# A decoder layer on one core: held-back gate products, a running sum in PSUM, low parts by adding transfers, and one more channel at seven products for eight

## The chip, the core and the metric

The kernel runs on one core of one Trainium2 chip. The core has a matrix engine (TensorE, PE here; the loading of its stationary operand has its own row, PEld), VectorE (DVE), ScalarE (ACT), GpSimd (POOL) and SyncE (SP), which issues most transfers from HBM. POOL issues the rest, among them all those that add what they bring to what is already in SBUF (the on-chip memory of 128 partitions). PE writes to PSUM, whose banks hold 512 float32 numbers for each partition.

The metric is the device time of one execution in microseconds; smaller is better. Beside it stands a profiled execution of the same program.

## What is computed

One layer over 512 tokens of 1024 channels: a normalisation, one wide input projection, two mixers (a convolution module A and gated linear attention B), a gated merge, an output projection with residual, and a feed-forward part. What the change touches, cut from the reference:

```python
u = _rmsnorm(h, norm1_g[l])
proj = u @ w_in[l]
a_glu, q, k, v, r, g_low, gate_a, gate_b = _split_cols(proj)
...
c = jax.nn.silu(_layernorm(c, conv_ln_g[l], conv_ln_b[l]))
...
o = o.reshape(bsz, seq, GLA_VDIM).astype(x.dtype) * jax.nn.silu(r)
y_gla = o @ w_gla_out[l]
merged = jax.nn.sigmoid(gate_a) * y_conv + jax.nn.sigmoid(gate_b) * y_gla
h = h + merged @ w_o[l]

u2 = _rmsnorm(h, norm2_g[l])
z = _causal_dwconv(u2 @ w_ffn_up[l], ffn_dw_w[l], ffn_dw_b[l])
h = h + (jax.nn.silu(z[..., :FFN_DIM]) * z[..., FFN_DIM:]) @ w_ffn_down[l]
```

D_MODEL is 1024, FFN_DIM 2816, and all inputs are float32.

## The kernel before

**Products in three passes.** Each operand is split into a high part, rounded to the type that PE multiplies fast (fp32r), and a low part, what the rounding left. A product is then three matmuls (`mm3`, L523): low x high, high x low, high x high. So PE needs a weight's low part first. `split_weight` (L400) makes both parts of the next weight in `order`: ACT casts the high part (L412, L442), and the low part is made in one of three ways. As a rule DVE subtracts (L413, L450). For the weights in the set `ADDED` (L47) ACT writes the negative of the weight, rounded, to the low tile (L444) and POOL issues a transfer that adds the weight from HBM once more (L445). Two early ones go to POOL. High and low tiles have four buffers each, raw weights four (`raw_tile`, L306). `weight` (L468) keeps the splits two entries ahead of use.

**Seven products for eight.** Where two halves of the tokens meet two halves of the channels, a Strassen-like scheme (steps a11, a12, s1, n2, s4, n3, a22) saves one product in eight for sums and differences of operands. `seven` (L1434) does it for whole weight blocks (w_r, w_o, w_down). `two_tiles` (L1325) does it for a pair of column tiles, a "two-product channel" in the feed-forward part: four weight parts x1, x3, x2, x4 (the first to the fourth), with steps a11 and a12, then n2 and s1, then n3 and s4, then a22. Each step is 12 matmuls of 256 tokens. A part's weights come from `two_sums` (L381): after the first part is split, POOL adds three half tiles (L384), after the second one more. The token sums that the steps take as the other operand (n2, s1, n3, s4) are made on DVE (L1288) and split there (L1301) in four rounds, one after each of the first channels (`some_sums`).

**The w_r stage.** `seven("w_r", ...)` makes the output gate r. `put_r` (L1525) takes each result from its bank: for a11, s1 and n2 ACT copies it to an r tile; for a12, s4 and n3 DVE combines bank and r tile (L1535), ACT applies silu (L1536) and DVE multiplies the attention output with it (L1537); for a22 ACT applies silu straight from the bank (L1531) and DVE multiplies. `gated_o` (L1229) then transposes the product on PE into one of three "ax" banks, from which ACT takes the high part and DVE the low part (L1241).

**Layer norm of branch A.** `ln_center` (L1014) subtracts the mean from one of eight channel tiles (DVE, L1015), squares it on ACT into a `btmp` tile (two buffers, L1017) and adds the square to a running sum, itself in the other `btmp` (DVE, L1021). This chain runs beside the merge's products (`pair_7`).

**The feed-forward part.** w_up has 44 column tiles, i and 22 + i for the two factors of channel tile i. `GROUPS` (L34) cuts the 22 channels into three groups of pairs; each group is made (up), then multiplied with its block of w_down. The first of a pair is gated, split and kept; the second is gated and combined with it (`first_gated` L1728, `second_of_pair` L1739). `up_plan` (L189) writes the order within a group: a plain channel is its two tiles of 24 matmuls of 512 tokens each, then its role; a unit mixes the four parts of one two-product channel with the tiles of a plain one. The main loop (L1830) walks this plan. In the first group channels 0 and 2 open, then 1, 3 and 4 are plain, then come units of channel 6 with plain 5 and of 7 with plain 8. When a two-product channel's last part is done, its value (the taps of the short convolution, silu) is begun at once.

**Order.** The text gives priorities; the builder puts each engine's instructions in a fixed order by these and by what it reckons will be ready. `tc.issue_after(x)` makes what is traced inside it follow x on x's engine; `tc.keep_in_program_order` does so among those it marks.

Of the kernel before, what the change touches and what calls it, by code (L numbers as in the profile page):

```python
# [10 lines left out]
F32 = mybir.dt.float32  # L11
# [6 lines left out]
P = 128  # L18
# [30 lines left out]
POOLED = {("w_qk", 0), ("w_qk", 1)}  # L49
ADDED -= POOLED  # L50
RATE = 5.0
ROWS = (0, 5, 5, 5, 8, 8, 8, 8)
# [48 lines left out]
def trunk_layer(ctx: ExitStack, tc: tile.TileContext, a: dict, out: bass.AP):  # L101
# [34 lines left out]
    def btmp():  # L136
        return tp.tile([P, T], F32, tag="btmp", name=nm("btmp"), bufs=2)
# [51 lines left out]
    def up_plan(gi):  # L189


        pairs = GROUPS[gi]
        whole = range(KT)

        def halves(*cuts):
            return [range(a, b) for a, b in zip((0, *cuts), (*cuts, KT))]

        def unit(q, f, kind):

            a, b = f, FT + f  # L200
            x1, x3, x2, x4 = (("part", q, part) for part in ("x1", "x3", "x2", "x4"))
            a1, a2 = (("tile", a, ks) for ks in halves(4))
            if kind == "opens":
                b1, b2, b3 = (("tile", b, ks) for ks in halves(4, 6))
                seq = [a1, x1, a2, x3, b1, x2, b2, x4, ("second", q), b3]
            elif kind == "closes":
                a1, a2, a3 = (("tile", a, ks) for ks in halves(3, 6))
                seq = [x1, a1, x3, a2, x2, a3, x4, ("second", q), ("tile", b, whole)]
            else:
                a1, a2 = (("tile", a, ks) for ks in halves(5))  # L210
                b1, b2 = (("tile", b, ks) for ks in halves(4))
                seq = [x1, a1, x3, a2, x2, b1, x4, ("second", q), b2]
            return seq + [("first", f)]

        firsts = [p for p, _ in pairs[1:]]
        if gi + 1 < len(GROUPS):
            firsts.append(GROUPS[gi + 1][0][0])
        plan = []
        n = 0
        if gi == 0:  # L220
            (p, q), (f, _) = pairs[1:3]
            for i, role in ((p, "first"), (q, "second"), (f, "first")):
                plan += [("tile", i, whole), ("tile", FT + i, whole), (role, i)]
            n = 2
        while n < len(firsts):
            last = n + 1 == len(firsts) and gi + 1 < len(GROUPS)
            kind = "closes" if last else "opens" if n == 0 else ""
            plan += unit(pairs[n][1], firsts[n], kind)
            n += 1
        if n < len(pairs):  # L230
            q = pairs[n][1]
            plan += [("tile", q, whole), ("tile", FT + q, whole), ("second", q)]
        return plan
# [97 lines left out]
    def load_block(name, pairs, step, d):  # L331
# [682 lines left out]
    def ln_center(k):  # L1014
        nc.vector.tensor_tensor(conv[k], stat["mean"], conv[k], ALU.add)  # L1015
        sq = btmp()
        nc.scalar.activation(sq, conv[k], AF.Square)  # L1017
        if k == 0:
            stat["sq"] = sq
        else:  # L1020
            nc.vector.tensor_tensor(stat["sq"], stat["sq"], sq, ALU.add)  # L1021

# [494 lines left out]

    rt = {}
    urgent += s4 + of_s4 + n3 + of_n3
# [5 lines left out]
    def put_r(step, t, n, acc):  # L1525
        if step in ("a11", "s1", "n2"):
            rt[t, n] = rp_.tile([P, T], F32, tag="r", name=nm("r"), bufs=8)
            return nc.scalar.copy(rt[t, n], acc)
        if step == "a22":
            rt[t, n] = rp_.tile([P, T], F32, tag="r", name=nm("r"), bufs=8)  # L1530
            nc.scalar.activation(rt[t, n], acc, AF.Silu)  # L1531
        else:
            r = rt[t, n]
            one, two = (r, acc) if step == "n3" else (acc, r)
            done = nc.vector.tensor_tensor(r, one, two, ALU.add if step == "a12" else ALU.subtract)  # L1535
            nc.scalar.activation(r, r, AF.Silu)  # L1536
        nc.vector.tensor_tensor(ot[t, n], ot[t, n], rt[t, n], ALU.mult)  # L1537
        return done if step == "n3" else None
# [289 lines left out]
    banks, values, units = {}, {}, {}  # L1828
    third = []
    for gi, pairs in enumerate(GROUPS):  # L1830
# [26 lines left out]
        for what, i, *rest in up_plan(gi):  # L1857
# [7 lines left out]
            if what == "part":  # L1865
# [115 lines left out]
```

## Time and profile before

| | us |
|---|---|
| median of 3 runs | 820.95 |
| lowest to highest | 820.51 to 821.41 |
| the profiled execution | 821.88 |
| its span | 820.2 |
| PE busy, share of the span | 808.7, 99% |
| DVE | 707.2, 86% |
| ACT | 488.2, 60% |
| POOL | 196.8, 24% |

The span goes from the first instruction to the last. An engine's busy time is the union of its instructions; matmuls overlap in their pipeline, so their rate is read from start to start and not from their durations. In the list of waits a row names who waited for whom, then the total, the times and the longest. In a timeline each row has the start, the time taken, engine, line, operation, what is written from what, the shapes and how many; what stands in brackets is the idle time before it and who ended it. In a table by stretches each engine has its busy time and its count. The stages in the profile: start and first projections to 245 us, w_r to 290, merge to 410, w_o to 466, and the three groups of the feed-forward part from 471, 609 and 701 us to the end.

### The profile page before, as it was taken

The numbers are of one execution on the slowest core, as the hardware profiler recorded it, in microseconds if no ns is written. First come the engines' busy times: TensorE is split into PE (matmuls) and PEld (weight loads), VectorE is DVE, ScalarE is ACT, GpSimd is POOL, SyncE is SP. The second block draws the span as 40 slices with busy tenths as digits, with TensorE's granted clock in tenths as the row PEclk, the third lists the DMA queues.
The fourth block names the chain that finished last, engine by engine and source line by source line (L and its number), as shares of the span: only waits on it lengthen the run. The fifth ranks groups of instructions, "written<-read, shape, count | busy, mean of one in ns | idle before, by whom it ended". The sixth has DMA issues, their size and how long they took to land.

```text
span 820.2 us, 11465 instructions
## 1 busy us (share of the span) xinstructions
PE 808.7 (99%) x4227; PEld 695.5 (85%) x4227; DVE 707.2 (86%) x1105; ACT 488.2 (60%) x744; POOL 196.8 (24%) x176
## 2 busy tenths in 40 slices
PE   9999999999999999999999999999999999999996
PEld 8888888888888788889988898898889988899885
DVE  6879999998999878595789889979975999689895
ACT  6667788677547574384445646556435663466554
POOL 2025433332203332122001100230123311522012
PEclk9999999999999999999999999999999999999999
DMA  8488858655831332433458613146632346335662
GB/s 327 153 193 177 190 161 178 157 123 134 183 96 36 96 111 95 129 103 103 155 106 227 201 58 103 52 159 166 140 130 92 143 121 167 103 103 178 156 129 103
DMA packets 36472, 113.60 MB, mean 139 GB/s; under 512 B 3688, under 2 KB 8944, under 8 KB 36416
## 3 DMA queue, kind: packets, MB, share of 16 engines
q1 hardware_dynamic: 28912, 86.39, 31.0%
q0 software_dynamic: 7488, 26.48, 18.9%
q8 instruction: 33, 0.54, 0.3%
q14 instruction: 23, 0.19, 0.1%
q10 hardware_dynamic: 16, 0.00, 0.0%
HBM read 110.76 MB, written 2.10 MB: 138 GB/s over the span
## 4 chain that ended last, share of the span: by engine, by line
PE 62%; DVE 1%; ACT 0%; issue 0%; POOL 0%; POOLq 0%; ACTq 0%
PE mm L527 14%; PE mm L528 14%; PE mm L529 14%; PE cv L527 4%; PE cv L528 4%; PE cv L529 4%; PE ax L529 2%; PE ax L527 2%; PE ax L528 2%; DVE btmp L1021 0%; PE ax L608 0%; PE ax L1233 0%; DVE wlo L413 0%; ACT junk L1778 0%; DVE hres L1485 0%
## 5 line engine op out<-in xcount | busy, mean ns | idle before, releaser
L527 PE MATMUL mm<-uh,wlo 128*128 128x512 f32 (+1 forms) x532 | 194.0, 365 | 0.7 <-DVE tmp L1335 0.7
L528 PE MATMUL mm<-ul,whi 128*128 128x512 f32 (+1 forms) x532 | 191.5, 360 | 0.0
L529 PE MATMUL mm<-uh,whi 128*128 128x512 f32 (+1 forms) x532 | 191.5, 360 | 0.0
L413 DVE TENSOR_TENSOR wlo<-raw,whi 128x1024 fp32r<-128x1024 f32 x82 | 96.8, 1186 | 30.4 <-ACT whi L412 26.6
L384 POOL TENSOR_TENSOR raw<-raw,raw 128x512 f32<-128x512 f32 x39 | 59.8, 1534 | 239.5 <-DVE wlo L413 107.3
L527 PEld LDWEIGHTS mm<-uh,wlo 128*128 128x128 f32 x532 | 100.5, 189 | 16.5 <-DVE tmp L1335 1.1
L529 PEld LDWEIGHTS mm<-uh,whi 128*128 128x128 f32 x532 | 100.4, 189 | 15.3
L528 PEld LDWEIGHTS mm<-ul,whi 128*128 128x128 f32 x532 | 100.5, 189 | 14.8
L442 ACT CAST whi<-raw 128x1024 fp32r<-128x1024 f32 x80 | 83.5, 1048 | 30.4 <-PE mm L529 13.3
L412 ACT CAST whi<-raw 128x1024 fp32r<-128x1024 f32 x82 | 78.9, 965 | 38.1 <-PE mm L529 23.1
L450 DVE TENSOR_TENSOR wlo<-raw,whi 128x1024 fp32r<-128x1024 f32 x50 | 66.2, 1328 | 7.2 <-ACT whi L442 7.1
L412 ACT CAST whi<-kept 128x1024 fp32r<-128x1024 f32 (+1 forms) x40 | 40.2, 1007 | 30.2 <-DVE kept L360 15.7
L413 DVE TENSOR_TENSOR wlo<-kept,whi 128x1024 fp32r<-128x1024 f32 (+1 forms) x40 | 47.9, 1201 | 5.5 <-ACT whi L412 5.5
L887 DVE SCALAR_TENSOR_TENSOR aside<-cv,pp,aside 128x255 f32<-128x255 f32 (+6 forms) x112 | 52.1, 465 | 0.0
L887 DVE SCALAR_TENSOR_TENSOR c<-aside,btmp,c 128x247 f32<-128x247 f32 (+13 forms) x93 | 52.0, 564 | 0.0
L887 DVE SCALAR_TENSOR_TENSOR c<-cv,pp,c 128x247 f32<-128x247 f32 (+13 forms) x93 | 43.2, 464 | 1.4 <-ACT c L883 1.4
L444 ACT ACTIVATE wlo<-raw 128x1024 fp32r<-128x1024 f32 x28 | 29.4, 1059 | 19.0 <-PE mm L527 19.0
L1332 ACT COPY tmp<-mm 128x256 f32<-128x256 f32 x38 | 14.1, 370 | 34.0 <-PE mm L529 33.4
L1705 DVE SCALAR_TENSOR_TENSOR tmp<-mm,pp,tmp 128x511 f32<-128x511 f32 (+1 forms) x42 | 31.0, 741 | 2.6 <-ACT tmp L1702 2.5
L1705 DVE SCALAR_TENSOR_TENSOR tmp<-tmp,pp,tmp 128x511 f32<-128x511 f32 (+1 forms) x32 | 27.8, 887 | 0.4
L384 POOL TENSOR_TENSOR raw<-raw 128x512 f32<-128x512 f32 x13 | 26.4, 2032 | 0.0
L1485 DVE TENSOR_TENSOR hres<-hres,mm 128x512 f32<-128x512 f32 (+1 forms) x37 | 24.6, 673 | 2.1 <-PE mm L529 2.0
(499 smaller groups left out, 2092.9 us busy)
## 6 DMA issues: line engine op xcount, KB each, us to landing
raw<-in_w_up_dram SPq DMA_DIRECT2D x44, 512.0 KB, 3.6
raw<-in_w_glu_dram SPq DMA_DIRECT2D x16, 512.0 KB, 5.3
raw<-in_w_down_dram SPq DMA_DIRECT2D x15, 512.0 KB, 4.1
wlo<-in_w_glu_dram POOLq DMA_DIRECT2D x12, 512.0 KB, 7.0
kept<-in_w_down_dram POOLq DMA_DIRECT2D x10, 512.0 KB, 6.2
raw<-in_w_v_dram SPq DMA_DIRECT2D x8, 512.0 KB, 5.8
raw<-in_w_qk_dram SPq DMA_DIRECT2D x8, 512.0 KB, 6.3
raw<-in_w_gb_dram SPq DMA_DIRECT2D x8, 512.0 KB, 4.5
```

Source lines behind the costliest of these rows:

```text
L384: work = nc.gpsimd.tensor_tensor(out, x, y, ALU.add)
L412: nc.scalar.copy(hi, raw)
L413: two_low[:] = [nc.vector.tensor_tensor(lo, raw, hi.bitcast(F32), ALU.subtract)]
L442: nc.scalar.copy(hi, raw)
L444: pace[0] = nc.scalar.mul(lo, raw, -1.0)
L450: pace[0] = nc.vector.tensor_tensor(lo, raw, hi.bitcast(F32), ALU.subtract)
L527: nc.tensor.matmul(acc, ll, rh, start=first, stop=False, **kw)
L528: nc.tensor.matmul(acc, lh, rl, start=False, stop=False, **kw)
L529: nc.tensor.matmul(acc, lh, rh, start=False, stop=last, **kw)
L887: nc.vector.scalar_tensor_tensor(out[:, j:], x[:, : half_t - j], w, out[:, j:], ALU.mult, ALU.add)
L1485: done = nc.vector.tensor_tensor(hres[t, n][:, c], hres[t, n][:, c], acc[:, c], op)
L1705: nc.vector.scalar_tensor_tensor(z[:, s:], acc[:, : T - s], w[j], z[:, s:], ALU.mult, ALU.add)
```

## The change

1. `put_r` no longer multiplies by the gate at once. It keeps the pair (t, n) in a list, and the next call that combines a bank multiplies behind that combination; the a22 calls multiply what is kept, and the last one its own.
2. The r tiles get six buffers for eight, and the second block of w_r's step a22 gets a tile of its own ("rx", as large as the two) in place of a slot of the raw ring.
3. `ln_center` squares the first tile into an "ax" bank, which then holds the running sum; the last addition writes to a `btmp` tile.
4. Thirteen tiles of w_up join `ADDED`: 1, 23, 3, 25, 8 in the first group, 9, 31, 20 in the second, 35, 16, 39, 19, 41 in the third.
5. The plans stand in a table (`PLANS`). Those of the second and third group give the old order. In the first group channel 4 becomes a two-product channel, and a new unit "both" lays the parts of 4 and 6 around plain channel 5: x1 x3 of 4, half a tile of 5, x2, half a tile, x4, then the same for 6 with the second tile.
6. A first part that follows roles is moved ahead of them, and the value of a two-product channel is begun with its role and no longer with its last part.

```diff
+PLANS = (
+(("plain",1,3),("both",4,6,5),("closes",7,8)),(("opens",10,9),("",11,20),("closes",21,12)),(("opens",14,13),("",15,16),("",18,17),("plain",19)),)
...
+ADDED |= {("w_up", j) for j in (1, 23, 3, 25, 8, 9, 31, 20, 35, 16, 39, 19, 41)}
...
+        def both(p, q, f):
+
+            x1, x3, x2, x4 = parts(p)
+            y1, y3, y2, y4 = parts(q)
+            (a1, a2), (b1, b2) = cut(f, 4), cut(FT + f, 4)
+            return [*(x1, x3, a1, x2, a2, x4, y1, y3, role(p), b1, y2, b2, y4, role(q)), role(f)]
...
+        for n in range(1, len(plan)):
+            at = n
+            while plan[n][0] == "part" and plan[n][2] == "x1" and at and plan[at - 1][0] in ("first", "second"):
+                plan[at - 1], plan[at] = plan[at], plan[at - 1]
+                at -= 1
         return plan
...
         elif (name, step, d) == ("w_r", "a22", 0):
             dst = keep_tile(name)
+        elif (name, step, d) == ("w_r", "a22", 1):
+            dst = rp_.tile([P, D], F32, tag="rx", name=nm("rx"), bufs=1)
...
     def ln_center(k):
         nc.vector.tensor_tensor(conv[k], stat["mean"], conv[k], ALU.add)
-        sq = btmp()
+        sq = btmp() if k else ax_bank()
         nc.scalar.activation(sq, conv[k], AF.Square)
         if k == 0:
             stat["sq"] = sq
         else:
-            nc.vector.tensor_tensor(stat["sq"], stat["sq"], sq, ALU.add)
+            total = stat["sq"] if k < KT - 1 else btmp()
+            nc.vector.tensor_tensor(total, stat["sq"], sq, ALU.add)
+            stat["sq"] = total
...
-            rt[t, n] = rp_.tile([P, T], F32, tag="r", name=nm("r"), bufs=8)
+            rt[t, n] = rp_.tile([P, T], F32, tag="r", name=nm("r"), bufs=6)
...
-        nc.vector.tensor_tensor(ot[t, n], ot[t, n], rt[t, n], ALU.mult)
+        if step == "a22":
+            done = None
+        with tc.issue_after(done.ins) if done else ExitStack():
+            while gated:
+                i, j = gated.pop()
+                nc.vector.tensor_tensor(ot[i, j], ot[i, j], rt[i, j], ALU.mult)
+        gated.append((t, n))
+        if (step, t, n) == ("a22", 3, 0):
+            i, j = gated.pop()
+            nc.vector.tensor_tensor(ot[i, j], ot[i, j], rt[i, j], ALU.mult)
         return done if step == "n3" else None
...
                 done = next(units[i])
                 if done:
-                    values[i] = value(i, done[0])
-                    banks[FT + i] = (None, done[1])
-                    third = [taps_at[0], third_ahead()]
+                    found_parts[i] = done
+                    third = [third_ahead()]
+            if what in ("first", "second") and i in found_parts:
+                done = found_parts.pop(i)
+                values[i] = value(i, done[0])
+                banks[FT + i] = (None, done[1])
+                third.append(taps_at[0])
             if what == "first":
-                w = first_gated(i, values.pop(i), banks.pop(FT + i)[1])
-                if any(i in pair for pair in pairs):
-                    found = first_of_pair(w)
+                with ExitStack() as order_of:
+                    for ins in third:
+                        if ins:
+                            order_of.enter_context(tc.issue_after(ins.ins))
+                    w = first_gated(i, values.pop(i), banks.pop(FT + i)[1])
+                    if any(i in pair for pair in pairs):
+                        found = first_of_pair(w)
+                third = []
```

More of the change, by code (lines that the diff above doesn't have):

```diff
@@ L193, in up_plan, with parts, cut @@
         whole = range(KT)
[L195 to L202, printed above, removed]
+        def parts(q):
+            return [("part", q, part) for part in ("x1", "x3", "x2", "x4")]
+        def cut(m, *at):
+            return [("tile", m, range(a, b)) for a, b in zip((0, *at), (*at, KT))]
@@ L203, in unit, with turns, one @@
+        def turns(m, role):
+            return [("tile", m, whole), ("tile", FT + m, whole), (role, m)]
+        def one(q, f, kind):
+            x1, x3, x2, x4 = parts(q)
             if kind == "opens":
-                b1, b2, b3 = (("tile", b, ks) for ks in halves(4, 6))
-                seq = [a1, x1, a2, x3, b1, x2, b2, x4, ("second", q), b3]
+                (a1, a2), (b1, b2, b3) = cut(f, 4), cut(FT + f, 4, 6)
+                seq = [a1, x1, a2, x3, b1, x2, b2, x4, role(q), b3]
             elif kind == "closes":
-                a1, a2, a3 = (("tile", a, ks) for ks in halves(3, 6))
@@ L220, in up_plan @@
[L220 to L232, printed above, removed]
+                a1, a2, a3 = cut(f, 3, 6)
@@ new lines, in up_plan, with role @@
+        seconds = {q for _, q in pairs}
+        def role(i):
+            return ("second" if i in seconds else "first", i)
+        plan = []
+        for kind, *units in PLANS[gi]:
+            if kind == "plain":
+                for i in units:
+                    plan += turns(i, role(i)[0])
+            elif kind == "both":
+                plan += both(*units)
+            else:
+                plan += one(*units, kind)
+        for n in range(1, len(plan)):
[3 more added lines that the diff above has]
+                at -= 1
```

19 lines of the change are left out of this document (7 added, 12 removed).

## The prediction

> **What bounds the kernel now.** The page comes first: TensorE (PE) is busy for 99% of the span, so the time is the length of PE's instruction stream plus the little that it waits.
>
> ```profile
> span 820.2 us, 11465 instructions
> ...
> PE 808.7 (99%) x4227; PEld 695.5 (85%) x4227; DVE 707.2 (86%) x1105; ACT 488.2 (60%) x744; POOL 196.8 (24%) x176
> ```
>
> The list of waits, asked for PE alone, then names all that PE waits for past the start (a fourth row of 1.1 us belongs to the start-up, which the diff does not touch).
>
> ```profile
> PE cv L527 <- DVE r L1535: 1.5, 1, 1.5
> PE ax L1233 <- DVE h L1241: 1.0, 1, 1.0
> PE mm L527 <- DVE tmp L1335: 0.7, 1, 0.7
> ```
>
> All three are waits for VectorE (DVE), before 331 us, and in the feed-forward part, from 466 us on, PE never waits for anything that the list shows. So the change can win in two ways: fewer products, and these three waits, 3.2 us together. What it does to DVE, ScalarE (ACT) and GpSimd (POOL) counts only where it makes PE wait.
>
> **One more two-product channel (4).** Channel 4 was two plain tiles, 48 products of 512 columns; as a two-product channel it is seven steps of 12 products of 256 columns, 84. The timeline of PE gives both rates:
>
> ```profile
> 507.27 0.39 PE L527 MATMUL mm<-uh,wlo 128*128 128x512 f32 x1
> ...
> 529.03 0.28 PE L527 MATMUL cv<-uh,wlo 128*128 128x256 f32 x1
> ...
> 630.15 0.28 PE L527 MATMUL mm<-uh,wlo 128*128 128x256 f32 x1
> ...
> 633.02 0.40 PE L527 MATMUL mm<-uh,wlo 128*128 128x512 f32 x1
> ```
>
> From 507.27 to 529.03 lie 96 products of 512: 21.76 / 96 = 0.227 us each. From 630.15 to 633.02 lie 24 of 256: 2.87 / 24 = 0.120. So 48 x 0.2267 = 10.88 goes and 84 x 0.1196 = 10.05 comes: **0.8 us** off the path. The switches between widths stay four, so nothing is added there.
>
> Around it, DVE loses two low parts and gains three and a half, with four combinations; POOL gains four half-tile additions.
>
> ```profile
> 491.00:529.00 38.00, 38.00 (x169) 31.46 (x168) 37.81 (x49) 22.47 (x30) 4.61 (x3) 1.00 0.21 70
> ...
> 524.09 1.21 DVE L1301 TENSOR_TENSOR xq<-kept,gainq 128x1024 fp32r<-128x1024 f32 x1
> ...
> 533.73 0.41 DVE L1335 TENSOR_TENSOR tmp<-tmp,ax 128x256 f32<-128x256 f32 x1
> ...
> 535.08 1.21 DVE L413 TENSOR_TENSOR wlo<-raw,whi 128x1024 fp32r<-128x1024 f32 x1
> ...
> POOL raw L384 <- DVE wlo L450: 42.2, 1, 42.2
> ```
>
> DVE: (3.5 - 2) x 1.21 + 4 x 0.41 = 3.5 us more, in a stretch where it is busy for 37.81 of 38 us. Against it the five low parts of this group that leave DVE (1, 23, 3, 25, 8) give back 5 x 1.21 = 6.1. POOL had been idle for 42.2 us before the first addition here, so four more fit. The tight point is the activations' sums: channel 4's third part needs the last of them, and it comes 2.87 + 2.87 + 12 x 0.227 = 8.5 us after channel 3's second tile ends at 507.27 + 48 x 0.227 = 518.2, so at 526.6 for the first and 528.1 for the second step. The last sum is done at 524.09 + 1.21 = 525.3 now, and four low parts (4.8 us) leave the queue ahead of it. I cost this at nothing; should DVE get no relief it would still be 2.8 us early, and each further us of DVE delay is a us of PE.
>
> **Gate multiplications held back.** Three engines in the stretch of the first two waits:
>
> ```profile
> 265.88 3.95 SPq L292 DMA_DIRECT2D raw<-in_w_gb_dram  x2
> ...
> 273.74 3.53 POOL L384 TENSOR_TENSOR raw<-raw,raw 128x512 f32<-128x512 f32 x2 [14.86 <-DVE h L1537]
> 277.24 2.26 POOL L384 TENSOR_TENSOR raw<-raw 128x512 f32<-128x512 f32 x1
> ...
> 276.04 0.68 DVE L1535 TENSOR_TENSOR r<-mm,r 128x512 f32<-128x512 f32 x1
> 276.64 1.72 DVE L413 TENSOR_TENSOR wlo<-kept,whi 128x1024 fp32r<-128x1024 f32 x1
> 278.28 1.77 DVE L1537 TENSOR_TENSOR h<-h,r 128x512 f32<-128x512 f32 x1
> 279.97 0.67 DVE L1535 TENSOR_TENSOR r<-r,cv 128x512 f32<-128x512 f32 x1
> ...
> 286.39 2.02 DVE L413 TENSOR_TENSOR wlo<-raw,whi 128x1024 fp32r<-128x1024 f32 x1 [0.19 <-ACT whi L412]
> ...
> 288.94 0.74 DVE L1241 SCALAR_TENSOR_TENSOR h<-ax,pp,h 128x512 fp32r<-128x512 f32 x1
> ```
>
> PE waits for the read of bank cv at 279.97, and just ahead of that read stands a multiplication of 1.77 us that nobody is waiting for. Held back behind the read, it lets PE go on at about 279.0, that is without a wait. The w_r block that gets a tile of its own frees a slot of the raw ring, so the second w_gb load need not follow the first by 3.6 us (two issues in 3.95 us); POOL's additions, over 273.74 to 279.50, then come earlier, away from the reads. The row at 276.04, with one operand in a bank, took 0.68 us inside them, while rows with both operands in SBUF took 1.72 and 1.77.
>
> What is late next is the second wait: the fourth transpose needs an ax bank that line 1241 frees at 289.68, and DVE is nearly full up to there. PE arrives 1.5 us sooner; DVE arrives sooner by what it no longer loses (1.77 against 0.69 for an undisturbed multiplication, 1.72 against 1.21, and some idle time) so some 1.5 to 2. The pair is bounded by nothing (all of the first wait turns up in the second) and by 2.5 (both go). I take **1.7**: the first goes, the second stays mostly. With six r tiles for eight, only the last two reuse a tile, of products combined several steps before; cost nothing.
>
> **Squares in a bank.** The third wait:
>
> ```profile
> 324.01 3.00 POOL L384 TENSOR_TENSOR raw<-raw,raw 128x512 f32<-128x512 f32 x2 [13.55 <-ACT btmp L1017]
> ...
> 324.48 1.38 DVE L1021 TENSOR_TENSOR btmp<-btmp,btmp 128x512 f32<-128x512 f32 x1
> ...
> 328.02 1.77 DVE L1021 TENSOR_TENSOR btmp<-btmp,btmp 128x512 f32<-128x512 f32 x1
> ...
> 330.18 0.39 PE L527 MATMUL mm<-uh,wlo 128*128 128x256 f32 x1 [0.73 <-DVE tmp L1335]
> ```
>
> Beside POOL's additions two sums of squares took 1.38 and 1.77 us. With the total in a bank they should take the 0.68 of the row at 276.04: 0.7 + 1.1 = 1.8 us of DVE, more than the wait of 0.7; and a second SBUF buffer is free for the next square. Gain **0.7**, between nothing and 0.7.
>
> **Thirteen low parts by adding transfers.** Each trades a subtraction of about 1.2 us on DVE (the 50 of the page average 1.33) for an ACT multiplication, a POOL issue, and a transfer that lands later. No low part of w_up is made so now, so the price comes from other weights and from w_down in the same stage:
>
> ```profile
> L450 DVE TENSOR_TENSOR wlo<-raw,whi 128x1024 fp32r<-128x1024 f32 x50 | 66.2, 1328 | 7.2 <-ACT whi L442 7.1
> ...
> L444 ACT ACTIVATE wlo<-raw 128x1024 fp32r<-128x1024 f32 x28 | 29.4, 1059 | 19.0 <-PE mm L527 19.0
> ...
> 49.47 1.06 ACT L444 ACTIVATE wlo<-raw 128x1024 fp32r<-128x1024 f32 x1 [1.52 <-PE mm L527]
> ...
> 50.82 0.85 POOL L445 DMA_DIRECT2D wlo<-in_w_glu_dram  x1 [4.55 <-DVE aside L887]
> ...
> DMA to landing us min/median/max: 5.3/7.6/12.0
> ...
> kept<-in_w_down_dram POOLq DMA_DIRECT2D x10, 512.0 KB, 6.2
> ...
> 602.53 1.05 ACT L442 CAST whi<-raw 128x1024 fp32r<-128x1024 f32 x1
> ...
> 609.13 0.39 PE L527 MATMUL cv<-uh,wlo 128*128 128x512 f32 x1
> ...
> 626.14 1.05 ACT L442 CAST whi<-raw 128x1024 fp32r<-128x1024 f32 x1 [3.75 <-PE ax L529]
> ```
>
> The "DMA to landing" row is of all 28 adding transfers of line 445. A low part is thus ready 1.05 + 1.06 + 0.3 (from 49.47 + 1.06 to POOL's issue at 50.82) + 5.3 to 7.6 = 7.7 to 10.0 us after its high part is begun, where DVE gets by with 1.05 + 1.21. The issues take POOL 13 x 0.85 = 11 us of the 350 from 470 on, and additions behind an issue wait for its ACT multiplication too; POOL is a quarter busy. ACT gains 13 x 1.06 = 14 us at 60% busy. On plain tiles there is time: 1, 23, 3 and 25 are two tiles (10.9 us) ahead. But tile 20's high part is begun at 626.14, when PE frees the buffer, and PE multiplies by its low part first at 633.02: 6.9 us. Tile 9 has 609.13 - 602.53 = 6.6. Tiles 16 and 8 stand behind a first part as 20 does, so I give them 6.9 also. At the least landing these four are 0.8 + 1.1 + 0.8 + 0.8 = 3.5 us late, at w_down's 6.2 us 7.1, at the median of 7.6 near 13.
>
> [...]
>
> I still cost it at nothing in the likeliest case, for PE's order is not that of the loops:
>
> ```profile
> 684.41 0.39 PE L527 MATMUL mm<-whi,sl 128*128 128x512 f32 x1
> 684.64 0.39 PE L527 MATMUL cv<-whi,sl 128*128 128x512 f32 x1
> 684.87 0.46 PE L528 MATMUL mm<-wlo,sh 128*128 128x512 f32 x1
> ```
>
> Here one product of the next sum (cv) stands inside that of mm, so the stream was laid out by what would be ready. Behind each of the four tiles lies a part of 2.87 us whose operands do not need it; put first, it covers the least lateness and most of that at 6.2 us. If that cover is gone, the price is the 3.5 to 7.1 us.
>
> **The value begun with the next step** moves conversions and taps of ACT and DVE behind the next first part. PE's order and count stay, and a part's products (2.87 us) lie over the move: nothing.
>
> **Sum.** 0.8 + 1.7 + 0.7 + 0 + 0 = 3.2 us. The profiled execution took 821.9 us (its span of 820.2 and 1.7 around it), so 818.7; the median of the runs shown is 0.9 lower, so **817.7 us**.
>
> **The rivals.**
> *The low parts are late in order (slower).* The stream keeps the four tiles where they are and PE waits at each. For it: 6.6 and 6.9 us against 7.7 at the least. Against it: the row at 684.64. It decides from about 6.2 us of landing: 817.7 + 7.1 = 824.8; at 5.3 us 821.2, with part of the cover 819.5 to 822.
> *The first wait only moves.* DVE is full from 276 to 290, so the transposes wait 2.5 us instead of 1.0: 817.7 + 1.7 = 819.4. For it: DVE's rows follow each other without a gap. Against it: the lost 1.6 us beside POOL.
> *DVE falls behind in the first group.* Channel 4 asks for the sums 14 us sooner than channel 6 did (526.6 against 529.0 + 2 x 2.87 + 24 x 0.227 = 540.2). Should DVE's order put channel 4's work ahead of them, they come some 3.5 us later: 0.7 us of wait, 818.4.
>
> **How the numbers follow.** Against the median a run of this kernel tells 0.2%, 1.6 us, from no change: faster is below 819.3, slower above 822.6. Chances: forecast, with the third rival in it, 0.58; the wait moves 0.14 (half of it still faster); late low parts 0.28 (0.16 of it slower, 0.12 within). Faster 0.64, same 0.19, slower 0.17. The range goes from all waits gone (820.95 - 0.8 - 3.2 = 816.9, with 0.5 of scatter 816.4) to 823.0, inside the late case; its own range for the likeliest is 816.4 to 818.6.
>
> **What would show it.** Right: PE counts 4227 + 36 = 4263 products; the three rows of PE's waits are gone or the middle one alone is left; L450's subtraction counts 50 - 13 - 2 = 35, L444's multiplication 41. Wrong: PE rows ended by "DMA wlo<-in_w_up", or idle PE before tiles 8, 9, 16, 20, which would make it the first rival; a transposes' wait above 2 us would make it the second; a wait for L1301 near 525 us the third.

## The result, and the profile after

The changed kernel took 832.2 us (median of four, 830.79 to 835.9) against 821.18 us before (four, 820.51 to 821.88): a ratio of 1.0136, 95% interval 1.0118 to 1.0154. It is 11.0 us slower; the forecast was 3.2 us faster. Its profiled execution took 830.79 us. The page's head, to be held against the first two lines of the prediction:

```profile
span 829.1 us, 11578 instructions
...
PE 809.4 (98%) x4263; PEld 696.6 (84%) x4263; DVE 696.6 (84%) x1097; ACT 503.1 (61%) x763; POOL 211.3 (25%) x193
```

PE issues the 4263 products that were reckoned, and DVE is indeed relieved by 10.6 us; yet the span grew by 8.9 us. So the loss is time in which PE stands still, and the list of waits, asked for PE, names it (in total, times, longest):

```profile
PE mm L542 <- DMA wlo<-in_w_up_dram: 7.6, 4, 2.6
PE mm L542 <- ACT tmp L1349: 2.1, 1, 2.1
...
PE ax L1250 <- DVE h L1258: 0.7, 1, 0.7
PE cv L542 <- DMA wlo<-in_w_up_dram: 0.6, 1, 0.6
```

(The row left out is the start-up's.) In this execution only the transposes' wait is left of the three old ones, at 0.7 us: up to the feed-forward part things went as forecast, or a little better. There, where PE had not waited at all, five waits for an adding transfer have come (8.2 us) and one for an ACT copy out of a bank (2.1 us). The timeline shows where each stands. The DVE and ACT rows near 518 us belong to the copy, those of ACT, POOL and SP near 628 us to tile 20:

```profile
515.29 1.66 DVE L465 TENSOR_TENSOR wlo<-raw,whi 128x1024 fp32r<-128x1024 f32 x1
...
517.48 0.74 DVE L1731 SCALAR_TENSOR_TENSOR tmp<-mm,pp,tmp 128x510 f32<-128x510 f32 x1
...
518.31 0.63 ACT L1739 ACTIVATE tmp<-tmp 128x512 f32<-128x512 f32 x1 [2.94 <-DVE tmp L1731]
518.85 1.03 ACT L427 CAST whi<-raw 128x1024 fp32r<-128x1024 f32 x1
519.78 0.36 ACT L1349 COPY tmp<-mm 128x256 f32<-128x256 f32 x1
...
520.20 0.38 PE L542 MATMUL mm<-xq,wlo 128*128 128x256 f32 x1 [2.10 <-ACT tmp L1349]
...
609.65 0.50 PE L542 MATMUL mm<-uh,wlo 128*128 128x512 f32 x1 [1.58 <-DMA wlo<-in_w_up_dram]
...
626.57 1.06 ACT L459 ACTIVATE wlo<-raw 128x1024 fp32r<-128x1024 f32 x1 [3.51 <-PE ax L542]
627.53 1.03 ACT L457 CAST whi<-raw 128x1024 fp32r<-128x1024 f32 x1
628.03 0.88 POOL L460 DMA_DIRECT2D wlo<-in_w_up_dram  x1 [2.55 <-ACT wlo L459]
628.59 0.33 SPq L309 DMA_DIRECT2D raw<-in_w_up_dram  x1
635.99 0.50 PE L542 MATMUL mm<-uh,wlo 128*128 128x512 f32 x1 [2.14 <-DMA wlo<-in_w_up_dram]
...
718.04 0.50 PE L542 MATMUL mm<-uh,wlo 128*128 128x512 f32 x1 [2.62 <-DMA wlo<-in_w_up_dram]
...
732.31 0.50 PE L542 MATMUL mm<-uh,wlo 128*128 128x512 f32 x1 [1.30 <-DMA wlo<-in_w_up_dram]
...
765.40 0.50 PE L542 MATMUL cv<-uh,wlo 128*128 128x512 f32 x1 [0.60 <-DMA wlo<-in_w_up_dram]
```

The five are tiles 9, 20, 35, 16 and 39. For tile 20 the whole chain is in view: the negative at 626.57, the transfer's issue at 628.03, a 512 KB load that SP starts at 628.59 into the raw slot just freed, and PE going on only at 635.99. The rows of line 460 give the time from issue to landing, first over all thirteen, then for tile 20 alone, tile 16 alone and tile 8 alone:

```profile
DMA to landing us min/median/max: 5.2/7.7/9.6
...
DMA to landing us min/median/max: 7.9/7.9/7.9
...
DMA to landing us min/median/max: 7.1/7.1/7.1
...
DMA to landing us min/median/max: 5.5/5.5/5.5
```

Tile 8, behind which SP's next load starts 3 us later and not 0.6 us, lands in 5.5 us and makes nobody wait.

### The profile page after: what moved, and what is told of

It reads as the page before. It is cut to its first block, busy times and chain, and to the rows that moved or that the text cites. A ratio compares the mean times of both kernels' runs of the same rounds, so it can differ in the third digit from the quotient of the medians.

```text
span 829.1 us, 11578 instructions
## 1 busy us (share of the span) xinstructions
PE 809.4 (98%) x4263; PEld 696.6 (84%) x4263; DVE 696.6 (84%) x1097; ACT 503.1 (61%) x763; POOL 211.3 (25%) x193
## 4 chain that ended last, share of the span: by engine, by line
PE 62%; DVE 23%; issue 6%; DMA 5%; POOL 2%; ACT 2%; POOLq 0%; DVEq 0%; ACTq 0%; SPq 0%
PE mm L542 14%; PE mm L544 14%; PE mm L543 14%; DVE c L902 5%; DMA wlo<-in_w_up_dram 4%; DVE tmp L1731 4%; PE cv L542 3%; PE cv L543 3%; PE cv L544 3%; DVE wlo L428 3%; DVE aside L902 3%; PE mm L756 2%; POOL raw L399 2%; PE ax L542 1%; PE ax L544 1%
## 5 line engine op out<-in xcount | busy, mean ns | idle before, releaser
L542 PE MATMUL mm<-uh,wlo 128*128 128x512 f32 (+1 forms) x532 | 196.2, 369 | 7.6 <-DMA wlo<-in_w_up_dram 7.6
L428 DVE TENSOR_TENSOR wlo<-raw,whi 128x1024 fp32r<-128x1024 f32 x86 | 101.0, 1181 | 40.2 <-ACT whi L427 32.4
L399 POOL TENSOR_TENSOR raw<-raw,raw 128x512 f32<-128x512 f32 x42 | 64.4, 1533 | 192.1 <-DVE wlo L428 121.3
L427 ACT CAST whi<-raw 128x1024 fp32r<-128x1024 f32 x86 | 82.7, 965 | 36.7 <-PE mm L544 26.5
L457 ACT CAST whi<-raw 128x1024 fp32r<-128x1024 f32 x78 | 81.5, 1048 | 20.4 <-PE mm L544 14.2
L459 ACT ACTIVATE wlo<-raw 128x1024 fp32r<-128x1024 f32 x41 | 43.3, 1061 | 36.9 <-PE mm L542 19.1
L465 DVE TENSOR_TENSOR wlo<-raw,whi 128x1024 fp32r<-128x1024 f32 x35 | 45.0, 1294 | 5.7 <-ACT whi L457 5.5
L1731 DVE SCALAR_TENSOR_TENSOR tmp<-mm,pp,tmp 128x511 f32<-128x511 f32 (+1 forms) x46 | 34.1, 742 | 4.7 <-ACT tmp L1728 4.6
L1731 DVE SCALAR_TENSOR_TENSOR tmp<-tmp,pp,tmp 128x511 f32<-128x511 f32 (+1 forms) x36 | 32.8, 930 | 1.5 <-ACT tmp L1728 1.2
L1349 ACT COPY tmp<-mm 128x256 f32<-128x256 f32 x32 | 11.8, 370 | 33.5 <-PE mm L544 32.6
```

The costliest lines, as they stand in the source:

```text
L399: work = nc.gpsimd.tensor_tensor(out, x, y, ALU.add)
L427: nc.scalar.copy(hi, raw)
L428: two_low[:] = [nc.vector.tensor_tensor(lo, raw, hi.bitcast(F32), ALU.subtract)]
L457: nc.scalar.copy(hi, raw)
L459: pace[0] = nc.scalar.mul(lo, raw, -1.0)
L465: pace[0] = nc.vector.tensor_tensor(lo, raw, hi.bitcast(F32), ALU.subtract)
```

## The experiments

Five questions were put. All times are in us; "before" was run beside each on the same chip and had medians of 821.4 to 821.7. A median is of 4 to 11 executions.

| run | median | lowest to highest | ratio to before, 95% interval |
|---|---|---|---|
| gates_alone | 819.74 | 819.42 to 820.50 | 0.9977, 0.9968 to 0.9987 |
| squares_alone | 820.56 | 819.74 to 821.60 | 0.9989, 0.9981 to 0.9998 |
| gates_squares | 819.54 | 818.61 to 820.39 | 0.9974, 0.9964 to 0.9983 |
| value_next | 821.39 | 820.85 to 822.50 | 1.0002, 0.9993 to 1.0011 |
| channel4 | 828.19 | 826.60 to 828.65 | 1.0084, 1.0068 to 1.0099 |
| plan_alone | 825.47 | 824.13 to 826.17 | 1.0046, 1.0034 to 1.0059 |
| no_adds | 823.17 | 822.39 to 826.04 | 1.0024, 1.0014 to 1.0033 |
| adds_plain | 821.28 | 820.51 to 824.28 | 1.0002, 0.9991 to 1.0012 |
| adds_plain5 | 820.39 | 820.09 to 821.57 | 0.9988, 0.9979 to 0.9997 |
| adds_alone | 836.88 | 836.30 to 838.37 | 1.0187, 1.0172 to 1.0202 |
| shared_raw | 829.72 | 826.10 to 830.50 | 1.0090, 1.0070 to 1.0110 |
| halves | 824.92 | 824.10 to 827.34 | 1.0050, 1.0035 to 1.0065 |
| again1, again2, again3 | 837.03, 834.47, 831.79 | one execution each | none |

### Are the first three waits worth what was reckoned?

gates_alone is the kernel before with points 1 and 2 of the change (`put_r`, six r tiles, the "rx" tile) and nothing else.

> The kernel before with the held-back gate multiplications, six r tiles and the w_r block's own tile alone. Theory (the wait at 279 us goes and the next one stays mostly): 2.0 us less than before, 819 us. Rival (the first wait only moves to the transposes): within 0.5 us of before.

squares_alone has point 3 alone:

```diff
-        sq = btmp()
+        sq = btmp() if k else ax_bank()
...
-            nc.vector.tensor_tensor(stat["sq"], stat["sq"], sq, ALU.add)
+            total = stat["sq"] if k < KT - 1 else btmp()
+            nc.vector.tensor_tensor(total, stat["sq"], sq, ALU.add)
+            stat["sq"] = total
```

> The kernel before with the running sum of squares kept in a bank, and nothing else of the change. My theory: TensorE's 0.7 us wait for the last square of the layer norm goes and nothing takes its place: 820.3 us, or 1.0 us off where the gain of the full change over the gates (3.1 against 2.1 us by matching products) is all of it: 820.1. Rival: the gain of that stage came from the gates having let VectorE run ahead, and the bank alone gives nothing: 821.2 (within 0.3).

gates_squares has both, with the old order of the up projection and no new adding transfers.

> The kernel before with the held-back gate multiplications and the running sum of squares in a bank, without adding transfers and with the old order of the up projection. My theory: these two parts have their effects side by side, 1.7 and 1.1 us by their own runs, and the up projection is as before: 818.4 to 818.8, below both kernels. Rival: the second overlaps with the first (the layer norm's wait moved when VectorE ran ahead): 819.7.

The gates gave 1.7 us (819.74 against 821.46), the bank 1.1 (820.56 against 821.67), both together 1.8 (819.54 against 821.38) and not the 2.8 of the sum. PE's waits past the start in gates_alone, and the longest one in squares_alone and in gates_squares:

```profile
PE ax L1235 <- DVE h L1243: 0.7, 1, 0.7
PE mm L529 <- DVE tmp L1337: 0.7, 1, 0.7
```

```profile
PE cv L527 <- DVE r L1537: 1.4, 1, 1.4
```

```profile
PE cv L529 <- DVE r L1539: 1.4, 1, 1.4
```

Each edit takes its own wait away, but in the traced execution of both the wait for the read of bank cv is back at 1.4 us, although the multiplication still follows the read. The timelines of gates_alone and of gates_squares say why:

```profile
271.27 2.99 POOL L386 TENSOR_TENSOR raw<-raw,raw 128x512 f32<-128x512 f32 x2 [12.55 <-DMA raw<-in_w_gb_dram]
...
276.98 1.21 DVE L415 TENSOR_TENSOR wlo<-kept,whi 128x1024 fp32r<-128x1024 f32 x1
278.12 0.68 DVE L1537 TENSOR_TENSOR r<-r,cv 128x512 f32<-128x512 f32 x1
```

```profile
273.52 3.53 POOL L386 TENSOR_TENSOR raw<-raw,raw 128x512 f32<-128x512 f32 x2 [15.90 <-DMA raw<-in_w_gb_dram]
273.55 2.35 DVE L415 TENSOR_TENSOR wlo<-kept,whi 128x1024 fp32r<-128x1024 f32 x1 [1.21 <-ACT whi L414]
277.01 1.74 POOL L386 TENSOR_TENSOR raw<-raw 128x512 f32<-128x512 f32 x1
277.52 2.31 DVE L415 TENSOR_TENSOR wlo<-kept,whi 128x1024 fp32r<-128x1024 f32 x1
279.76 0.68 DVE L1539 TENSOR_TENSOR r<-r,cv 128x512 f32<-128x512 f32 x1
```

A w_gb load landed 2.2 us later, so POOL's additions ran to 278.75 instead of 276.50 and lay over both of DVE's low parts, which took 2.35 and 2.31 us (1.81 and 1.21 in gates_alone). The late load alone does not give the 1.4 us, though. In again2, the changed kernel once more (below), it landed later still, at 273.53, and PE waited only 0.28 us; there DVE's first low part started just ahead of POOL's first addition and took 1.23:

```profile
273.62 1.23 DVE L428 TENSOR_TENSOR wlo<-kept,whi 128x1024 fp32r<-128x1024 f32 x1 [1.20 <-ACT whi L427]
```

```profile
273.68 4.01 POOL L399 TENSOR_TENSOR raw<-raw,raw 128x512 f32<-128x512 f32 x2 [16.01 <-DMA raw<-in_w_gb_dram]
```

All 17 traces of this case sort by these two things. With the gates held back, PE does not wait where the load landed by 271.5 us (five traces), waits 0.3 us where it landed later and DVE's first low part started ahead of the POOL addition that it met (five), and 1.4 where POOL was ahead, by 0.03 us (gates_squares). With the gates as before the load lands at 273.1 us or later, and the wait is 1.4 to 1.65 us with POOL ahead (before, squares_alone, plan_alone, adds_alone) and 0.5 to 0.6 with DVE ahead (channel4, value_next). So the 1.5 us of the traced execution of before were one side of a race, and not a fixed price. Four of the nine executions of gates_squares took 818.6 to 818.8, as expected, the other five 819.5 to 820.4; that those four are the ones without this wait was not traced.

### What does the new order of the first group cost?

no_adds is the changed kernel without its thirteen adding transfers:

```diff
-ADDED |= {("w_up", j) for j in (1, 23, 3, 25, 8, 9, 31, 20, 35, 16, 39, 19, 41)}
```

> The changed kernel with its thirteen w_up tiles back on VectorE's subtraction; everything else of the change stays. Theory (late low parts): the five waits of the matrix engine for the adding transfers, 8.2 us by the list of waits and some 9.0 counted from start to start, go, and the kernel comes to 819 to 821 us, with the 2.1 us wait for ScalarE in the first group left or longer, since VectorE has thirteen subtractions more. Rival (the seventh two-product channel and the new plan are what is slow): the time stays above 826 us.

plan_alone is the kernel before with points 5 and 6 only.

> The kernel before with the new order of the up projection (channel 4 by two-product, its value begun with the next step), and neither the adding transfers nor the held-back gates nor the bank. My theory: the first group's VectorE falls behind, and waits of about 3.5 us for ScalarE and VectorE stand against a saving of 0.8 us in products: 823.5 to 824. Rival: the waits of the first group in the run without adding transfers came from the gates or the bank, and the order alone saves its 0.8 us: 820.4.

channel4 is plan_alone with point 6 taken back: the value is begun where it was begun before, and no first part is moved ahead of roles (that part of its edit is not shown). value_next is plan_alone with the old contents of the first group:

```diff
-                    found_parts[i] = done
-                    third = [third_ahead()]
+                    values[i] = value(i, done[0])
+                    banks[FT + i] = (None, done[1])
+                    third = [taps_at[0], third_ahead()]
```

```diff
-(("plain",1,3),("both",4,6,5),("closes",7,8))
+(("plain",1,3,4),("",6,5),("closes",7,8))
```

> The kernel before with channel 4 by two-product in the new order of the first group, but each two-product channel's value begun where it was begun before (right after the last part of its product). Theory that the 3.8 us of the new order come from channel 4's extra sums and splits on VectorE and ScalarE in the first group: 824 to 825.5. Rival, that they come from beginning the values with the next step: 820.4 (the 0.8 us saved).

> The kernel before with every two-product channel's value begun with the next step, and channel 4 still by three products. If the loss of the new order is channel 4's: 821.0 to 821.5. If it is the later value's, in all three groups: 824 to 825.5.

The order alone costs 3.8 us (825.47 against 821.67) where 0.8 had been forecast as gain, and it is all channel 4: without it point 6 changes nothing (821.39 against 821.38), and with it point 6 is a help, since channel4 alone loses 6.8 us. Of the expectations only value_next's was met; plan_alone and channel4 lost 1.5 and 2.7 us more than the most that was expected. PE's waits of plan_alone in the first group, and then the longest of channel4:

```profile
PE mm L539 <- DVE wlo L425: 1.5, 2, 1.1
PE cv L539 <- ACT tmp L1344: 1.5, 1, 1.5
```

```profile
PE mm L534 <- DVE wlo L457: 2.6, 1, 2.6
PE mm L534 <- ACT tmp L1339: 1.2, 2, 0.8
```

no_adds has the first two of these again, at 1.5 us each; so the 823.17 of no_adds are the 819.54 of gates_squares and 3.6 us for the order. Neither side of its expectation (819 to 821, or above 826) came out: the waits for transfers are gone, and the order's own are back.

The products do get shorter, as was reckoned. From the first product of w_up to the first of w_down PE took 99.17 us in the trace of before, and 98.89 in that of halves (below), which has the new order and one wait of only 0.2 us there. It is the waits that outweigh this.

### Which adding transfers hurt, and which help?

adds_alone is the kernel before with the thirteen and nothing else, adds_plain the changed kernel with the first four only, adds_plain5 the same with tile 5 too:

```diff
+ADDED |= {("w_up", j) for j in (1, 23, 3, 25, 8, 9, 31, 20, 35, 16, 39, 19, 41)}
```

```diff
-ADDED |= {("w_up", j) for j in (1, 23, 3, 25, 8, 9, 31, 20, 35, 16, 39, 19, 41)}
+ADDED |= {("w_up", j) for j in (1, 23, 3, 25)}
```

```diff
+ADDED |= {("w_up", j) for j in (1, 23, 3, 25, 5)}
```

> The kernel before with the thirteen adding transfers alone. Theory (late low parts): the matrix engine waits at tiles 9, 20, 35, 16 and 39 as in the changed kernel, 8 to 9 us together, and at tile 8 little or not, since before the change its high part is begun 9 us ahead: 829 to 831 us. Rival (they are late only because the new plan moved VectorE and ScalarE): 820 to 823 us.

> The changed kernel with adding transfers for tiles 1, 23, 3 and 25 alone, the ones whose high parts are begun two tiles ahead. Theory (a lead below 8 us is what costs): no wait for a transfer is left, 819 to 821 us, the ScalarE wait of 2.1 us stays. Rival (transfers cost wherever they stand, by sharing the DMA engines with the weight loads): one third of the loss stays, 823 us or more.

> The changed kernel with the low parts of w_up tiles 1, 23, 3, 25 and 5 by adding transfers, those of the other eight on VectorE again. Theory that VectorE's 1.66 us low part of tile 5 stands ahead of the taps that ScalarE and then TensorE wait for at 518 us: the wait of 2.1 us falls to 0.5 or less, and the half clock behind it goes: 821.3 less 1.6 to 3.3, 818 to 819.7. Rival: ScalarE, which takes the negative of tile 5 in its place, is as late: 821.3 (within 0.5).

On the old order the thirteen cost 15.4 us (836.88 against 821.46; 829 to 831 had been expected), with PE waiting 9.2 us for them:

```profile
PE mm L528 <- DMA wlo<-in_w_up_dram: 5.0, 3, 2.7
PE cv L528 <- DMA wlo<-in_w_up_dram: 4.2, 2, 2.6
```

The expectation had left out the clock: two stretches of this trace run at half clock, which costs an estimated 3.4 us by what is worked out below, and the mean granted clock is 0.994 in all four executions, 0.998 in the trace of before. Two waits for DVE, of 1.0 and 0.8 us, which before does not have, come on top.

With the four of the plain tiles only, no wait for a transfer is left and the time is 821.28: these four save 1.9 us (from 823.17), and the two waits for a low part of DVE are gone; the other nine cost 10.9 (832.2 less 821.28). What adds_plain still waits for, and adds_plain5:

```profile
PE mm L542 <- ACT tmp L1349: 2.1, 1, 2.1
```

```profile
PE mm L542 <- ACT tmp L1349: 1.5, 1, 1.5
```

For the fifth, the mechanism held in sign and fell short in size. 1.66 us of low part left DVE's queue ahead of the tap, but a sum of line 1318 moved into part of the place, the tap ended only some 0.5 us earlier, and 0.9 us of time were won where 1.6 to 3.3 had been expected. Part of that is the clock: three of the ten executions of adds_plain, the traced one (823.12) among them, have a mean granted clock of 0.996, and none of adds_plain5 is below 0.997.

### Why do they land late, and is it the landing that counts?

shared_raw takes two loads away that start beside an adding transfer. It never loads tiles 42 and 38 and multiplies by 20 and 16 in their place, so it does not compute the layer:

```diff
+            if name == "w_up" and j in (FT + 20, FT + 16):
+                raws.append(raws[order.index((name, j - FT))])
+                return
             raw = raw_tile()
             nc.sync.dma_start(raw, a[name][j])
```

> The changed kernel in which w_up tiles 42 and 38 are not loaded (tiles 20 and 16 stand in for them, so the products of these two take other weights), so that no 512 KB load starts right behind the adding transfers of 20 and 16. Theory that the load beside it makes the landing late: these two land in 5.2 to 5.5 us instead of 7.9 and 7.1, and TensorE's waits on them (2.4 and 1.5 us of gap) shrink to 0.3 or less: 832.2 less 3 to 4, about 828.5. Rival, that an adding transfer of that stage takes 7 to 8 us by itself: waits stay, 832 (within 1).

halves cuts each transfer in two:

```diff
-                nc.gpsimd.dma_start(lo, a[name][spec], accum_op=ALU.add)
+                if name == "w_up":
+                    for c in (slice(0, T), slice(T, D)):
+                        nc.gpsimd.dma_start(lo[:, c], a[name][spec][:, c], accum_op=ALU.add)
+                else:
+                    nc.gpsimd.dma_start(lo, a[name][spec], accum_op=ALU.add)
```

> The changed kernel with each adding transfer of w_up issued as two of 256 KB, by column halves. Theory that TensorE stands on the time the whole tile takes to land: the first half lands some 1.5 to 2 us earlier and TensorE begins with it, so of the 11 us of gaps 4 to 7 go: 825 to 828. Rival, that the time is set by the queue's own steps and not by the bytes: the second half is later than the whole was, and the time is the same or up to 2 us longer: 832 to 834.

In shared_raw the transfers of tiles 20 and 16 land like this:

```profile
DMA to landing us min/median/max: 5.4/5.4/5.4
...
DMA to landing us min/median/max: 5.5/5.5/5.5
```

And of PE's waits for tiles in an mm bank two are left, those for tiles 9 and 35:

```profile
PE mm L545 <- DMA wlo<-in_w_up_dram: 4.4, 2, 2.5
```

From 7.9 and 7.1 us to 5.4 and 5.5, and PE's two waits of 2.14 and 1.30 are gone: the load that starts half a microsecond behind the transfer makes it late. The median gained 2.5 us of the 3 to 4 expected.

halves came out at 824.92, 7.3 us below the change. Its waits for the transfers:

```profile
PE mm L546 <- DMA wlo<-in_w_up_dram: 3.5, 4, 1.5
```

3.5 us are left of 8.2: PE begins with the half that landed first. For the five late tiles the first half lands 6.1 to 8.4 us after its issue, where the whole took 7.0 to 9.4. The second half, counted from the same issue, lands 0.3 to 1.7 us later than the whole did. So half the bytes did not take half the time here, and the rival was right about the second half; what helps is that its reader need not wait for it. The 4.7 us of these waits are not all of the 7.3: the wait for ACT's copy near 519 us is down from 2.1 to 0.2 too, for a reason that was not traced, and no stretch of this trace ahead of its end is at half clock.

### Where do the executions above 831 us come from?

The changed kernel once more, three times.

> The changed kernel itself, one execution with its trace. Theory that its executions above 831 us hold stretches of TensorE at half clock right behind a long wait: this execution takes about 830.8 us plus 1.7 us for each stretch of 3.413 us at clock 0.5 between 7 and 820 us of its trace (none: 830.8; one: 832.5; three: 835.9). Rival: longer executions have longer waits for the transfers at full clock.

> The changed kernel itself, a second execution with its trace: as for the first, 830.8 us plus 1.7 us for each stretch at clock 0.5 behind a wait; by the rival, no such stretch and longer waits.

> The changed kernel itself, a third execution with its trace: as for the first, 830.8 us plus 1.7 us for each stretch at clock 0.5 behind a wait; by the rival, no such stretch and longer waits.

again3, without a stretch at half clock in between, took 831.79 us (reckoned 830.8); again2 has two and took 834.47 (reckoned 834.2); again1 has three and took 837.03 (reckoned 835.9, and it also waited 1.3 us longer for tile 39, 1.9 against 0.6). So most of the extra microseconds are the half clock. The rival, longer waits for the transfers, accounts for the 1.3 us in again1, and about 1 us of scatter is left over. The table of stretches of again1, around its first and its second half-clock stretch (after the times come the length, the busy time of PE, PEld, DVE, ACT and POOL with counts, the granted clock, the DMA share and GB/s):

```profile
518.07:521.48 3.41, 1.35 (x11) 1.15 (x10) 3.41 (x5) 2.68 (x5) 0.00 (x0) 1.00 0.73 257
521.48:524.89 3.41, 3.41 (x18) 3.41 (x17) 3.41 (x6) 0.71 (x2) 2.14 (x2) 0.50 0.02 6
...
716.04:719.45 3.41, 1.48 (x13) 1.28 (x11) 1.50 (x4) 2.21 (x4) 0.00 (x0) 1.00 1.04 264
719.45:722.87 3.42, 2.72 (x6) 2.15 (x7) 1.20 (x1) 0.00 (x0) 2.34 (x2) 0.50 0.40 161
```

The third stretch follows, from 722.87, at 0.50 too. Reckoned as half of 3.413 us lost, an estimate, a stretch at clock 0.50 puts 1.7 us on the time; half of 3.413 in some 830 us is 0.002 off the mean clock. The four executions of the result agree within 1 us: 830.79, 830.91, 833.49 and 835.9 us had mean granted clocks of 0.998, 0.998, 0.996 and 0.992, by that reckoning none, none, one and three such stretches.

## Why the prediction was wrong

**The step that failed is the cost of the thirteen adding transfers.** The prediction worked out that tiles 9, 20, 16 and 8 would be late by 3.5 us at the least landing and 7.1 at w_down's, and then put nothing into the sum, because one row (684.64) showed a product of another bank inside a sum and PE's stream was therefore taken to be laid out by readiness. It was not, where it mattered: at each late tile PE stands in the loop's order until the transfer has landed, and the five waits are 8.2 us by the list. The first rival, at 824.8 us, was the right mechanism. It too fell short, for reasons that the runs show:

- *Which tiles.* 35 and 39 stand behind parts just as 20 does and wait 2.62 and 0.60 us; neither was counted. Tile 8 was counted and didn't wait.
- *The landing.* The rival went by 6.2 us. With a load started right behind them these transfers take 7.0 to 9.4, and at tiles 9, 20 and 16 the load beside is no chance: ACT reads the raw tile twice, the first time for the negative, which releases the transfer, and right behind it for the high part, which frees the raw slot that SP fills next (the rows from 626.57 to 628.59). shared_raw showed for two tiles that this load costs the time.
- *The order on ACT.* The prediction put 1.05 us for the high part ahead of the negative. At tiles 8, 9, 20, 16 and 39 ACT wrote the negative first (626.57 against 627.53), so tile 20's low part would have been ready 1.06 + 0.40 + 5.4 = 6.9 us after ACT began, which is in time, as shared_raw confirms. That the rival's 7.1 us of lateness lie so near the 8.2 of the list is thus in part luck: this term too long, the landing too short, one tile too many and two too few.
- *The clock.* A long wait could cost more than itself here, by the estimated 1.7 us for each stretch at half clock behind it: again1 had three and took 837.03 us, again3 none and 831.79 (the section on the hardware).

**Channel 4 and the value** were costed at a gain of 0.8 and at nothing, on the ground that the last token sum would be early by 2.8 us. A gain in products is there (98.89 against 99.17 us, with a wait inside), and the sums were not what came late. ACT's copy out of a bank, which PE needs for the next step, stood behind a silu that waited for DVE's tap, one term of the short convolution (the rows from 515.29 to 520.20), and elsewhere a part's low tile came late from DVE. The third rival named the cause, a DVE that falls behind in the first group, at 0.7 us of wait; plan_alone puts the whole at a loss of 3.8 where 0.8 was to be gained. The prediction did say that five low parts would relieve DVE: the first four of them won back 1.9 us. It looked at one consumer of a full engine, when every consumer of that engine moves.

**The gates** were sized at 1.7 and gave 1.7 by themselves. That the r wait goes and the transposes' stays mostly was right; the reason given, POOL's additions away from the reads, turned out to be a condition that depends on when a load lands and on which of DVE and POOL starts first. That 1.7 came out so exactly is in part luck: the wait that it was sized by is 0.5 to 0.6 us in two other traces with the old gates.

**The squares** were sized at 0.7 and gave 1.1 by themselves, with an interval of 0.2 to 1.6 that holds the forecast. Gates and squares together gave 1.8 where 2.4 had been reckoned.

From before to the change the runs make a chain, each a step further: gates and squares together -1.8, the new order +3.6, four transfers -1.9, nine transfers +10.9. (Steps of a chain add up by themselves; their 10.8 differ from the 11.0 measured by what before took beside each.) Of the 10.9 for the nine, the waits of the traced execution are 8.2 us by the list and 9.0 counted from start to start, and 1.4 lie between it and the median, where the half clock of other executions enters; the other 0.5 were not traced further.

The best kernel found is gates_squares, with 819.54 us about a quarter per cent below before; gates_alone cannot be told from it.

## What to carry to other kernels

Where the trace gives a lead and a landing time, and the landing is the longer, put the difference into the sum; an order that might be rearranged is a hope until the trace shows it for that very tile. Here a transfer that started when a buffer was read landed late beside the refill of that buffer (7.9 and 7.1 us, 5.4 and 5.5 without it); cost such a one by landings with a load beside them, and try it in pieces if its reader can begin with a piece (halves: 824.92 us against 832.2). When an engine is full, ask of all that wait on it, at one remove too, which comes late next.

## What the hardware showed beyond that

**TensorE's granted clock was 0.50 behind each of nine stretches in which PE was busy for 1.48 us or less.** In the 17 traces of this case the granted clock changed only on a grid of 3.413 us, whose place differs from one execution to the next. Take the grid's stretches at full clock, those that begin in the last 10 us of a trace left out. Where PE was busy for 1.48 us or less, the next stretch had clock 0.50: nine of nine. With 1.61 to 2.38 us it kept 1.00: 28 of 28. At the end of all 17 traces, when PE's work runs out, the clock falls behind a stretch with 1.50 us or less as well. Stretches of the change's profile and of shared_raw that kept it:

```profile
713.59:717.00 3.41, 1.83 (x16) 1.63 (x14) 1.82 (x3) 2.21 (x5) 0.00 (x0) 1.00 1.04 267
717.00:720.41 3.41, 2.37 (x10) 1.97 (x11) 1.23 (x1) 0.30 (x1) 1.98 (x2) 1.00 0.48 185
```

```profile
715.97:719.38 3.41, 1.61 (x7) 1.34 (x8) 1.23 (x1) 1.17 (x2) 1.31 (x1) 1.00 0.72 247
719.38:722.79 3.41, 3.41 (x26) 3.15 (x25) 0.42 (x1) 0.00 (x0) 2.70 (x3) 1.00 0.00 0
```

The same wait of the change, 2.62 us for tile 35, fell across two stretches in its first trace and cost nothing more; in again1 most of it lay in one (1.48 us busy) and the clock halved. At half clock, a stretch with 2.72 us of busy PE left it there; 3.27 and 3.41 brought it back. By this most of the 5 us are accounted for over which the changed kernel's four executions spread, with mean granted clocks of 0.992 to 0.998; those of before spread over 1.4.

**In the changed kernel's trace three adding transfers landed in 5.2 to 5.5 us, and the other ten, each with another transfer close by, in 7.0 to 9.6.** That a load behind it is the cause was tested for two tiles (shared_raw: 5.4 and 5.5 us where it had been 7.9 and 7.1); the rest is read from the traces. In the changed kernel's, tiles 1, 3 and 8, whose next 512 KB load starts 1.2, 1.5 and 3.0 us behind the issue, land in 5.2, 5.2 and 5.5 us. Tiles 9, 20, 16 and 35, whose next load starts within 0.6 us, take 7.0, 7.9, 7.1 and 8.1. Tiles 23 and 25, issued 2.9 and 1.9 us behind another adding transfer that was still under way, take 8.5 and 7.8. In adds_alone a load starts 0.4 us ahead of tile 3's transfer, and it takes 8.9 us and not 5.2. The share of the DMA engines is 1.04 in the stretch from 713.59, in which tile 35's transfer and loads run side by side.

**Of a DVE low part and a POOL addition that overlapped near 273 us, the one that started first kept its time.** Both read and write SBUF here. In the stretch near 273 us of all 17 traces the low part of `wlo<-kept,whi` took 1.23 us in the seven where it started 0.00 to 0.09 us ahead of a POOL addition, and that addition took 2.3 to 2.4. In the five where POOL's first addition started 0.03 to 0.24 us ahead, the addition took 1.3 us and the low part 2.1 to 2.35. A few hundredths of a microsecond thus decided 1.1 us of DVE there, and by that most of PE's wait for bank cv.
